# Moving the overflow branch, the router's order and three smaller edits in a two-layer attention and expert kernel

## The chip, the cores and the metric

The kernel runs on one core of a Trainium2 chip. The metric is the device time of one execution in microseconds. A core has five engines that run their own instruction streams and wait for each other through semaphores: TensorE (PE in the rows; PEld are its weight loads, which overlap the products), VectorE (DVE), ScalarE (ACT), GpSimd (POOL) and SyncE (SP), which here only issues DMA transfers. A `q` behind an engine's name (SPq, PEldq) marks an instruction of that engine's sequencer: a DMA issue, a register load, a branch, a semaphore.

## The reference, cut to what matters

512 tokens of 1024 numbers go through two layers. Each layer is a mixer (two kinds of attention and an output projection) and a mixture of 16 experts, each followed by a layer norm:

```python
for l in range(DEPTH):                        # 2
    mix = hybrid_mixer(x, w_in[l], ...)
    x = layer_norm(ALPHA * x + mix, ln1_g[l], ln1_b[l])
    ffn = grouped_moe(x, router_w, router_bias, w_gate[l], w_up[l], w_down[l])
    x = layer_norm(ALPHA * x + ffn, ln2_g[l], ln2_b[l])
# grouped_moe
aff = sigmoid(xt @ router_w)                  # 512 x 16
biased = aff + router_bias
group_score = sum of the two largest of biased in each of 4 groups of 4 experts
g_sel = argmax(group_score); e_idx = the two largest of biased inside group g_sel
gates = aff at e_idx, divided by their sum
out = sum over experts of gates * (silu(xt @ w_gate) * (xt @ w_up)) @ w_down
```

## The kernel before, in words

Most of the kernel is written for a planner that orders each engine's instructions by the order in which they are traced, takes a later one where an engine would otherwise be free, and draws the semaphores. Two places are ordered by hand with `tc.manual_schedule`: the end of the mixer and router (lines 764 to 817, for VectorE, ScalarE and TensorE) and the end of a layer.

**Router.** The tokens are four tiles of 128. For tile t, `residual` adds the mixer's output, `turn` transposes the sum through TensorE, and `logits` (line 652) multiplies it with the router's weights in eight steps of 128 rows, two half tiles of four steps; each float32 step shows as two records. `wgb` holds the router's weights, 16 columns of a step beside 16 columns of another product. `scores` finishes the logits with mean and deviation (L695, L696). `route` (line 860) chooses on VectorE, for two tiles at once, the group and the two experts (L885 to L914, many small operations that depend on each other), and counts the tokens ahead of each with small TensorE products (L921); `R["pos"]` (L924) is each token's place in its expert's list. `centre` and `scaled` (L689, L701) write the normed rows x1, which are stored to DRAM (`xdr`). `places` makes, from the positions, a matrix that picks expert 0's tokens, and `gather(t, i)` (L722) collects, transposed, half i of the columns of expert 0's rows out of tile t by TensorE. All four tiles of a half must be in before the half is complete. Twelve small products (`warm`, L200) have no use but to keep TensorE at work.

**Overflow.** An expert's list holds 128 tokens. `route_count` takes the largest position, over partitions by a TensorE transposition, into an integer `cmi`. `overflow` (line 1170) loads it into a register of every engine (L1172) and branches (L1175) over a loop that would compute the surplus tokens; with these inputs the loop is skipped. On the skipping path each engine increments its own semaphores by what the skipped code would have done, and SyncE does so for the semaphores of eight DMA lanes.

**Experts.** For each of 16 experts `gate_up` multiplies 128 gathered rows with the gate and up weights in eight pieces. The weights come by SyncE in loads of 1 MB (`load_gu` four, `load_wd` two per expert) into 12 `big` buffers. ScalarE copies each piece to a rounded part (L163) and VectorE subtracts to get the rest (L164, for expert 0 also L731 and L736 in `first_hi` and `first_lo`), into four `hl` buffers; each piece then takes three pairs of products (L1061, L1062). `down` (L1083) does the same with the down weights. `between` holds what is traced ahead of a piece. Rows of experts from 1 on are gathered by GpSimd (`fetch`, an indirect DMA, L1025) into `xg`, from lists made by `listed` and `index`, and are transposed and split by `rows_T`. Results of experts 0 to 12 are scattered to DRAM (`ydr`). Those of experts 13 to 15 (`LATE` = 13) stay on the chip; `late_rows` prepares their way back and multiplies out the gates of the expert's tokens (L1119), read by L1122. `parts` (L1092, L1093) takes a late expert's result out of its banks. The eight PSUM banks have three names: four `mm`, two `tr`, two `pv`. The down-projection uses two `pv`, one for each half of the columns.

What stands between the router and the experts before:

```python
fetch(1)
with tc.issue_after(r["counted"]):      # the cast of the count
    pre["lo"](2); pre["lo"](3)
with tc.manual_schedule(engines={SP}):
    overflow(l, r)
    pre["gu", 2] = load_gu(l, 2)
```

Of the kernel before, what the change touches and what calls it, by code (L numbers as in the profile page):

```python
# [8 lines left out]
F32 = mybir.dt.float32  # L9
# [5 lines left out]
OP = mybir.AluOpType  # L15
# [80 lines left out]
def block_kernel(ctx, tc, xT0, x0, win, wqk, wuv, wo, gvec, lnp, rw, rb, wgu, wdn, consts, angles, stripd, rowsd, out):  # L96
# [36 lines left out]
    def u4(name, dt=F32):  # L133
        return sl.tile([128, 1024], dt, name=name, tag="u4", bufs=NU4)
# [18 lines left out]
    def ps(tag):  # L153
        return psp.tile([128, 512], F32, name=tag, bufs={"mm": 4, "tr": 2, "pv": 2}[tag])
# [3 lines left out]

    nlo = [0]

    def split(hi, lo, src, eng=None):

        i = nc.scalar.copy(hi, src).ins  # L163
        (eng or nc.vector).tensor_sub(lo, src, hi.bitcast(F32))  # L164
        return i
# [65 lines left out]
    def attention(l, xh, xl, wraw, first, rest, x_dram):  # L231
# [373 lines left out]

        wgb = u4("wgb")[:, :256].rearrange("p (a b c) -> p a b c", a=8, b=2)
        for j in range(2):
# [44 lines left out]
        def logits(t, i):  # L652

            if i == 0:
                pls[t] = ps("pv")
            for k in range(4 * i, 4 * i + 4):
                R["pe"] = nc.tensor.matmul(pls[t][:, :NE], xts[t][i][:, (k % 4) * 128:(k % 4 + 1) * 128],
                                           wgb[:, k, 0, :], start=(k == 0), stop=(k == 7)).ins

# [38 lines left out]
        def scaled(t, a, b_):  # L698
            c = slice(a * 512, b_ * 512)
            x1 = pre["x1"][t]  # L700
            nc.vector.scalar_tensor_tensor(x1[:, c], x1[:, c], rss[t], b[:, c], op0=OP.mult, op1=OP.add)  # L701
            if b_ == 2:
                (nc.sync if t == NT - 1 else nc.scalar).dma_start(xdr[l][t * 128:(t + 1) * 128, :], x1)

        def norm(t):
# [58 lines left out]
        with tc.manual_schedule(engines={E.DVE, E.Activation, E.PE}):  # L764
# [18 lines left out]
            turn(3, 0)  # L783
            R["warm"] = ps("tr")
            turn(3, 1)
            logits(3, 0)
            gather(0, 0)
            logits(3, 1)
            scores(2)
            centre(3, 0, 1)  # L790
            scores(3)
            first_hi(2)
            centre(3, 1, 2)
            gather(0, 1)
            gather(1, 0)
            gather(1, 1)
            warm(6, R["warm"], R["pe"])

# [8 lines left out]
            places(3)  # L807
            cm = route_count(R)
            scaled(2, 1, 2)
            scaled(3, 0, 1)  # L810
            scaled(3, 1, 2)
            gather(2, 0)
            gather(2, 1)
            cm()
            gather(3, 0)
            gather(3, 1)
# [9 lines left out]
    def load_gu(l, e, part=None, after=None):  # L826
        ws = []
        for k in range(4) if part is None else (part,):
            w = bigt()
            i = nc.sync.dma_start(w, wgu[l, e, :, 2048 * k:2048 * (k + 1)]).ins  # L830
            if after is not None:
                tc.add_manual_dep(i, after.name, mybir.DependencyInfo(mybir.DependencyClass.Sync,
                                                                      mybir.DependencyReason.DATA),
                                  reason="small transfers first")
            ws.append(w)
        return ws if part is None else ws[0]
# [23 lines left out]
    def route(R, lg, ta, tb, while_placing=lambda: None):  # L860
# [16 lines left out]
        def v16(t):  # L877
# [14 lines left out]
        gs = st(G)  # L892
        nc.vector.reduce_max(gs, pr, axis=AX.X)
        gs4 = gs.rearrange("p (t g) -> p t g", t=n)
        mx = st(n)
        nc.vector.reduce_max(mx, gs4, axis=AX.X)
        ge = st(G)
        ge4 = ge.rearrange("p (t g) -> p t g", t=n)
        nc.vector.tensor_tensor(ge4, gs4, mx[:, :, None].to_broadcast([128, n, 4]), op=OP.is_equal)
        nc.vector.tensor_mul(ge, ge, C("gw", 0, G))  # L900
        nc.vector.reduce_max(mx, ge4, axis=AX.X)
        nc.vector.tensor_tensor(ge4, ge4, mx[:, :, None].to_broadcast([128, n, 4]), op=OP.is_equal)

# [3 lines left out]
        bi = b4[:, :, None, :].to_broadcast([128, G, 4, 4])  # L907
        nc.vector.tensor_tensor(v4(t1), bi, bj, op=OP.is_ge)
        nc.vector.tensor_tensor(v4(t2), bi, bj, op=OP.is_gt)
        nc.vector.tensor_mul(v16(t1), v16(t1), lt)  # L910
        nc.vector.tensor_max(t1, t1, t2)
        rk = st()
        nc.vector.reduce_sum(rk, t1.rearrange("p (a b) -> p a b", b=4), axis=AX.X)
        nc.vector.scalar_tensor_tensor(sel.rearrange("p (g j) -> p g j", j=4), rk.rearrange("p (g j) -> p g j", j=4),  # L914
                                       1.5, ge[:, :, None].to_broadcast([128, G, 4]), op0=OP.is_lt, op1=OP.mult)
# [11 lines left out]
    def route_count(R):  # L927

        cm = sm.tile([128, 2], F32, name="cs")
        nc.vector.reduce_max(cm[:, 0:1], R["pos"], axis=AX.X)  # L930

        def over_tokens():
            pm = ps("tr")
            nc.tensor.transpose(pm[0:1, 0:128], cm[:, 0:1], ident)
            nc.vector.reduce_max(cm[0:1, 1:2], pm[0:1, 0:128], axis=AX.X)
            R["counted"] = nc.vector.tensor_copy(R["cmi"][0:1], cm[0:1, 1:2]).ins

        return over_tokens

# [40 lines left out]
    def ffn_plain(l, e, xg):  # L980


        def piece(w, k):
            t = u4("wp")
            nc.sync.dma_start(t, w[l, bass.ds(e, 1), :, k * 1024:(k + 1) * 1024].rearrange("o p m -> p (o m)"))
            return t
# [22 lines left out]
    def experts(l, r, pre):  # L1009
# [100 lines left out]
        def late_rows(e):  # L1110
# [5 lines left out]
            nc.scalar.copy(ohT, transpose4(of, 0))  # L1116
            p = ps("pv")
            for t in range(NT):
# [5 lines left out]

        fetch(1)
        with tc.issue_after(r["counted"]):
            pre["lo"](2)
            pre["lo"](3)
        with tc.manual_schedule(engines={mybir.EngineType.SP}):
            overflow(l, r)  # L1130
            pre["gu", 2] = load_gu(l, 2)
        st[0] = {}
        rows_T(0, 0)
        rows_T(0, 1)
        for e in range(NE):
# [12 lines left out]
            if e == 1:  # L1148
                between[4] = lambda: fetch(3)
            if e and e + 3 < NE:  # L1150
# [19 lines left out]
    def overflow(l, r):  # L1170
# [4 lines left out]
        with tc.If(cnt > CAP):  # L1175
# [15 lines left out]
            with tc.For_i(0, NE, 1) as e:  # L1191
                oe = sm.tile([128, 1], F32, name="o_oe", bufs=1)
                with tc.For_i(0, NT, 1) as t:
                    nc.sync.dma_start(oe, od[bass.ds(e, 1), :, bass.ds(t, 1)].rearrange("o p m -> p (o m)"))
                    oi = sm.tile([128, 1], I32, name="o_oi", bufs=1)
                    nc.vector.tensor_copy(oi, oe)
                    xr = u4("xr")
                    nc.sync.dma_start(xr, xdr[l].rearrange("(t p) d -> t p d", p=128)[bass.ds(t, 1)].rearrange(
# [294 lines left out]
```

## Time and profile before

| what | value |
|---|---|
| three timed runs | median 1224.01 us (1220.31 to 1225.26) |
| profiled execution | 1224.46 us, span 1222.7 us |
| TensorE busy | 1160.0 us, 95% |
| VectorE, ScalarE, GpSimd busy | 84%, 66%, 24% |
| mean granted clock of TensorE | 0.974 |
| HBM | 267.96 MB read, 31.98 MB written |

All times in rows are microseconds from the start of the span unless marked ns. In a timeline row stand the start, the duration, the engine, the line, the operation, the tiles written and read (out<-in) and their shapes; neighbours of one kind are merged and counted (x8). In brackets is the idle time of the engine before, and what ended it. A granted clock of 1.00 is the level of 2.4 GHz, 0.50 that of 1.2 GHz. The ends of matmuls are modelled.

### The profile page before, as it was taken

Reading aid. Unit: us, or ns where it says so; the run is one execution under the profiler, and the core shown is the slowest. Engines: PE = TensorE matmul, PEld = TensorE weight load, DVE = VectorE, ACT = ScalarE, POOL = GpSimd, SP = SyncE. Lnnn points to the kernel's source line nnn. Section 1 sums busy time; section 2 is a strip of 40 time slices with the busy share of each in tenths; the row PEclk is TensorE's granted clock in tenths of the full one; section 3 lists DMA queues with packets and bytes.
Section 4 is the critical chain, followed back from the end, with each engine's and each line's share of the span. In section 5 each row is a group of like instructions: output and inputs, shape, how many; then the busy total and the mean of one; then the engine's idle time right before and its main releaser. Section 6 shows DMA issues by size and latency. Waiting matters only on the chain. (4 is left out here: it accounts for less than half of the span.)

```text
span 1222.7 us, 16875 instructions
## 1 busy us (share of the span) xinstructions
PE 1160.0 (95%) x5753; PEld 910.2 (74%) x5753; DVE 1027.7 (84%) x1859; ACT 802.6 (66%) x1264; POOL 298.5 (24%) x237
## 2 busy tenths in 40 slices
PE   8998899999999999999898998999989999999995
PEld 6686556787788888887686765568878888888873
DVE  4599967488999999988957998665789999999887
ACT  4533668344888888887545346773448888888873
POOL 2336332210111111200543443322102111112004
PEclk8999999998999999999999999999889999999998
DMA  7626004465999999987236160145479999999741
GB/s 253 199 71 231 29 18 147 162 226 231 377 380 389 390 376 381 373 325 282 87 130 175 50 237 1 70 138 184 161 291 378 391 380 393 382 372 365 293 172 69
DMA packets 56972, 292.21 MB, mean 239 GB/s; under 512 B 10063, under 2 KB 13903, under 8 KB 28464
## 3 DMA queue, kind: packets, MB, share of 16 engines
q1 hardware_dynamic: 47376, 270.48, 60.0%
q0 software_dynamic: 8064, 15.36, 3.5%
q10 hardware_dynamic: 1440, 5.24, 1.1%
q8 instruction: 47, 0.77, 0.3%
q14 instruction: 45, 0.37, 0.1%
HBM read 267.96 MB, written 31.98 MB: 245 GB/s over the span
## 5 line engine op out<-in xcount | busy, mean ns | idle before, releaser
L163 ACT CAST hl<-big 128x1024 fp32r<-128x1024 f32 x438 | 457.6, 1054 | 126.8 <-PE mm L1062 62.3
L164 DVE TENSOR_TENSOR hl<-big,hl 128x1024 fp32r<-128x1024 f32 x403 | 484.6, 1226 | 58.2 <-ACT hl L163 51.0
L1061 PE MATMUL mm<-hl,xh 128*128 128x512 f32 x504 | 207.4, 412 | 0.0
L1062 PE MATMUL mm<-hl,xh 128*128 128x512 f32 x504 | 197.4, 392 | 0.0
L1083 PE MATMUL pv<-hl,hT 128*128 128x512 f32 x720 | 172.6, 395 | 4.1 <-DVE big L1093 4.1
L1083 PEld LDWEIGHTS pv<-hl,hT 128*128 128x128 f32 x720 | 136.7, 190 | 33.7 <-DVE big L1093 4.8
L271 PE MATMUL mm<-big,hl 128*128 128x512 f32 (+1 forms) x624 | 142.7, 387 | 2.3 <-ACT hl L163 1.2
L271 PEld LDWEIGHTS mm<-big,hl 128*128 128x128 f32 x624 | 114.4, 195 | 28.0 <-ACT hl L163 2.9
L1025 POOL DMA_INDIRECT xg<-xdr,ii x30 | 52.4, 1746 | 288.2 <-DVE ii L1039 254.0
L164 POOL TENSOR_TENSOR hl<-big,hl 128x1024 fp32r<-128x1024 f32 x35 | 84.7, 2424 | 134.4 <-ACT hl L163 120.1
L1062 PEld LDWEIGHTS mm<-hl,xh 128*128 128x128 f32 x504 | 95.4, 189 | 16.0
L1061 PEld LDWEIGHTS mm<-hl,xh 128*128 128x128 f32 x504 | 95.2, 189 | 15.7
L1062 PE MATMUL mm<-hl,xl 128*128 128x512 f32 x252 | 98.8, 392 | 0.0
L1061 PE MATMUL mm<-hl,xl 128*128 128x512 f32 x252 | 98.7, 392 | 0.0
L633 PE MATMUL mm<-hl,big 128*128 128x512 f32 x384 | 94.6, 397 | 0.0
L492 ACT ACTIVATE P<-P,mn 128x128 f32<-128x128 f32 (+3 forms) x128 | 71.9, 568 | 18.6 <-DVE mn L490 16.5
L633 PEld LDWEIGHTS mm<-hl,big 128*128 128x128 f32 x384 | 70.3, 188 | 13.3
L504 ACT COPY big<-tr 128x512 f32<-128x512 f32 (+3 forms) x128 | 49.7, 431 | 36.5 <-PE tr L502 35.5
L502 PE MATMUL tr<-cn,P 128*128 128x128 f32 x320 | 61.8, 293 | 9.8 <-DVE P L498 9.3
L502 PEld LDWEIGHTS tr<-cn,P 128*128 128x128 f32 x320 | 36.0, 141 | 42.8 <-ACT big L504 17.1
L1103 POOL DMA_INDIRECT ydr<-y,ii x26 | 26.5, 1018 | 146.8 <-ACT y L1099 123.2
L572 POOL TENSOR_TENSOR mh<-dd,cn 128x256 f32<-128x256 f32 (+2 forms) x64 | 44.5, 717 | 66.1 <-DVE mn L490 39.8
(277 smaller groups left out, 1881.7 us busy)
## 6 DMA issues: line engine op xcount, KB each, us to landing
big<-wgu SPq DMA_DIRECT2D x128, 1024.0 KB, 7.6
big<-wdn SPq DMA_DIRECT2D x64, 1024.0 KB, 7.1
big<-win SPq DMA_DIRECT2D x10, 1024.0 KB, 5.6
ydr<-zz SPq DMA_DIRECT2D x2, 4096.0 KB
big<-wo SPq DMA_DIRECT2D x8, 1024.0 KB, 9.8
big<-ydr SPq DMA_DIRECT2D x8, 1024.0 KB, 4.9
big<-wqk SPq DMA_DIRECT2D x4, 1024.0 KB, 6.1
big<-dq SPq DMA_DIRECT2D x32, 128.0 KB, 2.3
```

Source lines behind the costliest of these rows:

```text
L163: i = nc.scalar.copy(hi, src).ins
L164: (eng or nc.vector).tensor_sub(lo, src, hi.bitcast(F32))
L271: nc.tensor.matmul(p[:, ts], w[j == 1][:, k * 128:(k + 1) * 128], x, start=(j + k == 0), stop=(j == end and k == 7))
L492: nc.scalar.activation(e, e, AF.Exp, bias=mn[:, i:i + 1], scale=-1.0, accum_out=su[:, i:i + 1])
L502: nc.tensor.transpose(p[:, (i - kb) * 128:(i - kb + 1) * 128], P[:, PO[i] + kb * 128:PO[i] + (kb + 1) * 128], ident)
L504: copies.append(nc.scalar.copy(pt[kb], p[:, :512 - 128 * kb]).ins)
L572: last_mask[0] = nc.gpsimd.tensor_tensor(m[:, c:c + w], dd, C("slope", h, h + 1).to_broadcast([128, w]), op=OP.mult)
L633: R["pe"] = nc.tensor.matmul(pp[t][i], x, w[:, i * 512:(i + 1) * 512], start=first, stop=last).ins
L1025: return nc.gpsimd.indirect_dma_start(out=st[e]["xg"], out_offset=None, in_=xdr[l], in_offset=bass.IndirectOffsetOnAxis(ap=st[e]["ii"][:, ...
L1061: nc.tensor.matmul(pg, x, w[:, :512], start=(k == 0 and x is a and w is wh), stop=last)
L1062: nc.tensor.matmul(pu, x, w[:, 512:], start=(k == 0 and x is a and w is wh), stop=last)
L1083: nc.tensor.matmul(py[i], x, w[:, i * 512:(i + 1) * 512], start=(k == 0 and x is a and w is wh), stop=last)
```

## The change

- Overflow: the branch moves from between router and experts into expert 14 (`LATE + 1`), ahead of piece 3 of its gate and up products. The count is taken ahead of piece 3 of expert 0.
- Router's products: `logits` multiplies with 128 columns instead of 16. The columns beyond the 16 wanted are those of neighbouring steps and zeros, and nobody reads their results; the zeros are set by GpSimd.
- Order of the router's end: the gather of tile 0's first half goes behind all logits, tile 1's second half behind the routing; `centre(3)` is one operation; the warm-up products go; the last gathers finish the first half of columns before the second.
- `route`: the same operations, with those that choose the group and those that rank the experts alternating.
- Second expert's gather: three of the four loads of the third expert's gate and up weights wait until GpSimd has issued the gather of expert 1 (`issued`, a small memset behind it). `first_lo` of pieces 2 and 3 goes behind the split of expert 0's rows.
- Rows of expert 1 are transposed ahead of piece 7 of expert 0 and piece 1 of expert 1 (before: 6 and 7).
- Gates' product in `late_rows`: bank `mm` instead of `pv`.
- Inside the branch: one weight buffer, and the scratch tile for the rows.

```diff
     def split(hi, lo, src, eng=None):
         i = nc.scalar.copy(hi, src).ins
-        (eng or nc.vector).tensor_sub(lo, src, hi.bitcast(F32))
+        last_lo[0] = (eng or nc.vector).tensor_sub(lo, src, hi.bitcast(F32)).ins
...
-        wgb = u4("wgb")[:, :256].rearrange("p (a b c) -> p a b c", a=8, b=2)
+        wgt = u4("wgb")
+        wgb = wgt[:, :256].rearrange("p (a b c) -> p a b c", a=8, b=2)
+        nc.gpsimd.memset(wgt[:, 256:384], 0.0)
...
-                R["pe"] = nc.tensor.matmul(pls[t][:, :NE], xts[t][i][:, (k % 4) * 128:(k % 4 + 1) * 128],
-                                           wgb[:, k, 0, :], start=(k == 0), stop=(k == 7)).ins
+                R["pe"] = nc.tensor.matmul(pls[t][:, :128], xts[t][i][:, (k % 4) * 128:(k % 4 + 1) * 128],
+                                           wgt[:, 32 * k:32 * k + 128], start=(k == 0), stop=(k == 7)).ins
...
             turn(3, 0)
-            R["warm"] = ps("tr")
             turn(3, 1)
             logits(3, 0)
-            gather(0, 0)
             logits(3, 1)
             scores(2)
-            centre(3, 0, 1)
+            centre(3)
             scores(3)
             first_hi(2)
-            centre(3, 1, 2)
+            gather(0, 0)
             gather(0, 1)
             gather(1, 0)
-            gather(1, 1)
-            warm(6, R["warm"], R["pe"])
...
             places(2)
             places(3)
-            cm = route_count(R)
+            scaled(3, 0, 1)
             scaled(2, 1, 2)
-            scaled(3, 0, 1)
+            gather(1, 1)
             scaled(3, 1, 2)
             gather(2, 0)
+            gather(3, 0)
             gather(2, 1)
-            cm()
-            gather(3, 0)
             gather(3, 1)
...
-        nc.vector.reduce_max(gs, pr, axis=AX.X)
...
         nc.vector.tensor_tensor(v4(t1), bi, bj, op=OP.is_ge)
+        nc.vector.reduce_max(gs, pr, axis=AX.X)
         nc.vector.tensor_tensor(v4(t2), bi, bj, op=OP.is_gt)
+        nc.vector.reduce_max(mx, gs4, axis=AX.X)
         nc.vector.tensor_mul(v16(t1), v16(t1), lt)
+        nc.vector.tensor_tensor(ge4, gs4, mxb, op=OP.is_equal)
         nc.vector.tensor_max(t1, t1, t2)
+        nc.vector.tensor_mul(ge, ge, C("gw", 0, G))
...
-            p = ps("pv")
+            p = ps("mm")
             for t in range(NT):
                 nc.tensor.matmul(p[:, 0:1], of[:, t * 128:(t + 1) * 128], r["gm"][:, t * NE + e:t * NE + e + 1],
...
-        fetch(1)
-        with tc.issue_after(r["counted"]):
-            pre["lo"](2)
-            pre["lo"](3)
-        with tc.manual_schedule(engines={mybir.EngineType.SP}):
-            overflow(l, r)
-            pre["gu", 2] = load_gu(l, 2)
+        fetched = fetch(1)
+        with tc.issue_after(fetched):
+
+            issued = nc.gpsimd.memset(sm.tile([128, 1], F32, name="gs"), 0.0)
         st[0] = {}
         rows_T(0, 0)
         rows_T(0, 1)
+        with tc.issue_after(last_lo[0]):
+            pre["lo"](2)
+            pre["lo"](3)
+        pre["gu", 2] = [load_gu(l, 2, k, issued if k else None) for k in range(4)]
...
-                between[5 if e else 6] = lambda: rows_T(e + 1, 0)
-                between[6 if e else 7] = lambda: rows_T(e + 1, 1)
+                between[5 if e else 7] = lambda: rows_T(e + 1, 0)
+                if e:
+                    between[6] = lambda: rows_T(e + 1, 1)
             if LATE - 1 <= e < NE - 1:
                 between[3] = lambda: late_rows(e + 1)
+            if e == LATE + 1:
+                between[3] = both(lambda: overflow(l, r), between[3])
             if e == 0:
+                between[3] = lambda: route_count(r)
                 between[4] = lambda: (route_rest(r), index(1, 1, 2))
-                between[6] = both(lambda: (listed(0), index(0, 1, 2)), between[6])
-                between[7] = both(lambda: fetch(2), between[7])
+                between[6] = lambda: (listed(0), index(0, 1, 2))
+                between[7] = both(between[7], lambda: fetch(2))
             if e == 1:
+                between[1] = lambda: rows_T(1, 1)
                 between[4] = lambda: fetch(3)
```

## Rows read from the trace of the kernel before

**Rows 1.** The page: busy us by engine; a costly group (busy, mean ns | idle before).

```profile
PE 1160.0 (95%) x5753; PEld 910.2 (74%) x5753; DVE 1027.7 (84%) x1859; ACT 802.6 (66%) x1264; POOL 298.5 (24%) x237
...
L164 DVE TENSOR_TENSOR hl<-big,hl 128x1024 fp32r<-128x1024 f32 x403 | 484.6, 1226 | 58.2 <-ACT hl L163 51.0
```

**Rows 2.** Waits of TensorE: us in total, times, longest.

```profile
PE mm L1061 <- ACT xh L163: 5.9, 2, 4.0
```

**Rows 3.** Timeline of layer 0, from tile 3's logits to expert 0.

```profile
273.08 1.06 PE L657 MATMUL pv<-wgb,xt 128*128 128x16 f32 x8 [0.24 <-ACT xt L650]
...
274.00 1.76 PE L722 MATMUL mm<-oh,x 128*128 128x128 f32 x8
...
277.32 0.23 DVE L695 SCALAR_TENSOR_TENSOR lg<-c,lnm,pv 128x16 f32<-128x16 f32 x1 [3.40 <-PE pv L657]
...
278.69 0.18 DVE L889 TENSOR_TENSOR route<-route 128x24 f32<-128x24 f32 x1
...
281.56 0.19 DVE L914 SCALAR_TENSOR_TENSOR r_sel<-route 128x32 bf16<-128x32 f32 x1
...
281.80 1.47 PE L200 MATMUL tr<-strip 128*128 128x256 bf16 x12
...
283.52 0.19 DVE L924 TENSOR_TENSOR r_pos<-pv,r_sel 128x32 f32<-128x32 f32 x1 [1.11 <-PE pv L921]
...
284.09 2.14 PE L722 MATMUL mm<-oh,x 128*128 128x128 f32 x16 [0.61 <-DVE oh L716]
...
289.42 1.07 ACT L163 CAST xh<-mm 128x512 fp32r<-128x512 f32 x2 [8.82 <-SPq L1175]
...
290.06 0.50 PE L1061 MATMUL mm<-big,xh 128*128 128x512 f32 x1 [1.90 <-ACT xh L163]
```

**Rows 4.** Timeline of layer 1, tile 3's logits and expert 0's first product.

```profile
877.60 1.10 PE L657 MATMUL pv<-wgb,xt 128*128 128x16 f32 x8 [0.24 <-ACT xt L650]
...
896.63 0.80 PE L1061 MATMUL mm<-big,xh 128*128 128x512 f32 x1 [3.96 <-ACT xh L163]
```

**Rows 5.** Stretches: length, busy us (instructions) by engine, granted clock, DMA share, GB/s.

```profile
270.90:274.30 3.40, 3.16 (x28) 2.92 (x28) 2.81 (x8) 1.85 (x3) 0.92 (x1) 1.00 0.95 304
274.30:281.20 6.90, 6.90 (x35) 6.90 (x34) 3.54 (x18) 2.81 (x5) 0.00 (x0) 0.51 0.02 5
284.60:288.00 3.40, 3.40 (x33) 3.35 (x32) 3.37 (x8) 0.00 (x0) 0.00 (x0) 1.00 0.62 248
291.30:294.80 3.50, 3.50 (x10) 2.67 (x10) 3.50 (x11) 1.08 (x2) 0.00 (x0) 0.51 0.95 371
...
895.50:902.40 6.90, 5.77 (x14) 4.47 (x15) 5.63 (x15) 2.96 (x4) 0.73 (x1) 0.51 0.79 297
```

**Rows 6.** Timeline of VectorE, routing of the first two tiles of layer 0.

```profile
257.61 0.17 DVE L889 TENSOR_TENSOR route<-route 128x24 f32<-128x24 f32 x1
...
259.30 0.15 DVE L901 TENSOR_REDUCE route<-route 128x2 f32<-128x8 f32 x1
```

**Rows 7.** Timeline of the stages of experts 14 and 15, layers 0 and 1.

```profile
560.85 4.61 PE L1083 MATMUL pv<-hl,hT 128*128 128x512 f32 x12 [2.06 <-DVE big L1093]
...
568.82 0.15 DVE L1122 COPY gs<-pv 128x1 f32<-128x1 f32 x1
...
576.18 2.89 PE L1083 MATMUL pv<-hl,hT 128*128 128x512 f32 x12
...
1167.10 4.23 PE L1083 MATMUL pv<-hl,hT 128*128 128x512 f32 x12 [2.06 <-DVE big L1093]
```

**Rows 8.** Branch lines: duration ns min/median/max, first and last start us.

```profile
L1172 PEldq TENSOR_LOAD <-r_cmi x2: 926/1006/1087, 287.1 to 891.9; - x2
...
L1175 PEldq COMPARE_BRANCH  x2: 328/340/352, 288.3 to 892.9; - x2
```

**Rows 9.** DMA issues of the page: KB each, median us to landing.

```profile
big<-wdn SPq DMA_DIRECT2D x64, 1024.0 KB, 7.1
```

**Rows 10.** Waits of SyncE's queue: us in total, times, longest.

```profile
SPq L830 <- DVE hl L164: 251.4, 88, 17.8
```

More of the change, by code (lines that the diff above doesn't have):

```diff
@@ L157, in bigt @@
         return big.tile([128, 2048], dt, name="big")
-    nlo = [0]
+    nlo, last_lo = [0], [None]
     def split(hi, lo, src, eng=None):
         i = nc.scalar.copy(hi, src).ins
-        (eng or nc.vector).tensor_sub(lo, src, hi.bitcast(F32))
+        last_lo[0] = (eng or nc.vector).tensor_sub(lo, src, hi.bitcast(F32)).ins
         return i
@@ L700, in scaled @@
             x1 = pre["x1"][t]
-            nc.vector.scalar_tensor_tensor(x1[:, c], x1[:, c], rss[t], b[:, c], op0=OP.mult, op1=OP.add)
+            i = nc.vector.scalar_tensor_tensor(x1[:, c], x1[:, c], rss[t], b[:, c], op0=OP.mult, op1=OP.add).ins
             if b_ == 2:
                 (nc.sync if t == NT - 1 else nc.scalar).dma_start(xdr[l][t * 128:(t + 1) * 128, :], x1)
+            return i
         def norm(t):
@@ L831, in load_gu @@
             if after is not None:
-                tc.add_manual_dep(i, after.name, mybir.DependencyInfo(mybir.DependencyClass.Sync,
+                tc.add_manual_dep(i, after.ins.name, mybir.DependencyInfo(mybir.DependencyClass.Sync,
                                                                       mybir.DependencyReason.DATA),
-                                  reason="small transfers first")
+                                  reason="rows first")
             ws.append(w)
@@ L892, in route @@
         gs = st(G)
-        nc.vector.reduce_max(gs, pr, axis=AX.X)
         gs4 = gs.rearrange("p (t g) -> p t g", t=n)
-        mx = st(n)
-        nc.vector.reduce_max(mx, gs4, axis=AX.X)
-        ge = st(G)
+        mx, ge = st(n), st(G)
         ge4 = ge.rearrange("p (t g) -> p t g", t=n)
[L899 to L902, printed above, removed]
+        mxb = mx[:, :, None].to_broadcast([128, n, 4])
         t1, t2 = st(4 * W), st(4 * W)
@@ L908, in route @@
         nc.vector.tensor_tensor(v4(t1), bi, bj, op=OP.is_ge)
+        nc.vector.reduce_max(gs, pr, axis=AX.X)
         nc.vector.tensor_tensor(v4(t2), bi, bj, op=OP.is_gt)
+        nc.vector.reduce_max(mx, gs4, axis=AX.X)
         nc.vector.tensor_mul(v16(t1), v16(t1), lt)
+        nc.vector.tensor_tensor(ge4, gs4, mxb, op=OP.is_equal)
         nc.vector.tensor_max(t1, t1, t2)
+        nc.vector.tensor_mul(ge, ge, C("gw", 0, G))
         rk = st()
         nc.vector.reduce_sum(rk, t1.rearrange("p (a b) -> p a b", b=4), axis=AX.X)
+        nc.vector.reduce_max(mx, ge4, axis=AX.X)
+        nc.vector.tensor_tensor(ge4, ge4, mxb, op=OP.is_equal)
         nc.vector.scalar_tensor_tensor(sel.rearrange("p (g j) -> p g j", j=4), rk.rearrange("p (g j) -> p g j", j=4),
@@ L930, in route_count @@
         nc.vector.reduce_max(cm[:, 0:1], R["pos"], axis=AX.X)
[L932 to L938, printed above, removed]
+        pm = ps("tr")
+        nc.tensor.transpose(pm[0:1, 0:128], cm[:, 0:1], ident)
+        nc.vector.reduce_max(cm[0:1, 1:2], pm[0:1, 0:128], axis=AX.X)
+        nc.vector.tensor_copy(R["cmi"][0:1], cm[0:1, 1:2])
     def second(a2, t1, sel):
@@ L980, in ffn_plain @@
     def ffn_plain(l, e, xg):
+        t = u4("wp")
         def piece(w, k):
-            t = u4("wp")
             nc.sync.dma_start(t, w[l, bass.ds(e, 1), :, k * 1024:(k + 1) * 1024].rearrange("o p m -> p (o m)"))
@@ L1196, in overflow @@
                     nc.vector.tensor_copy(oi, oe)
-                    xr = u4("xr")
+                    xr = scr
                     nc.sync.dma_start(xr, xdr[l].rearrange("(t p) d -> t p d", p=128)[bass.ds(t, 1)].rearrange(
```

## The prediction

> **What bounds the kernel now.** I read the busy times first, then TensorE's waits, then the timeline and the granted clock of the two places that the change touches, in both layers. TensorE is busy 1160.0 of 1222.7 us [rows 1]; all its gaps together are some 63 us, so a gain must come from a named gap or from a stretch at the low clock. In the waits the reader is to see that its longest single wait is 4.0 us, for ScalarE's copy of the first expert's rows; it comes once per layer [rows 2]. The timeline of layer 0 shows its cause: the gathers run from 284.09, then the count is taken, every engine goes through the overflow branch, and ScalarE's copy is released by SyncE's semaphores of that branch (L1175) at 289.42; expert 0's products start at 290.06 after 1.90 us of nothing [rows 3]. In layer 1 the same gap is 3.96 us, up to 896.63 [rows 4]. The granted clock is 0.51 (the 1.2 GHz level for nearly all of it) from 274.3 to 281.2 and again after each gap, from 291.3 and from 895.5; in between, over the gathers from 284.6, it is 1.00 [rows 5].
>
> **The change, part by part.** The sum is made against the profiled execution's own 1224.46 us (span 1222.7), which is 0.45 above the median shown.
>
> Router, both layers. Now: eight records of tile 3's first logits from 273.08, a gather of eight records at 0.22 us each (low clock), the other logits, so that VectorE's L695 starts at 277.32 [rows 3]. The gather goes behind the logits, so these start at 274.0. What 128 columns cost: eight 16-wide records take 1.06 us, sixteen 128-wide gather records 2.14 [rows 3], 0.133 against 0.134 each; the weight loads set the pace in both. Below, the difference could be zero, above, 0.01 us for each of the 64 records of a layer; I take 0.3 us a layer, 0.6 in all. The clock I take as full here, because the 128-wide gathers of 284.6 to 288.0 kept it full while the stretch before the fall, 3.16 of 3.40 us busy but largely 16-wide, did not [rows 5]. Then the logits end at 274.0 + 8 x 0.13 = 275.1.
>
> The Trainium skill, "TensorE: Matmul & The Clock Gate", section "What's actually happening", lets the clock follow how busy the engine has been. Read as busy time, that speaks against the widening: the engine was busy before the fall as well. By it the low clock stays at the router, and that is the first rival, priced below from rows.
>
> L695 to L889 is 1.37 us today [rows 3] and stays so. L889 to the end of L914 is 3.06 [rows 3], with each dependent step waiting for the last. The new order alternates two chains; the scheduler already did so in the first half's routing, where L889 to L901 took 1.69 us [rows 6]. With two more steps of 0.2 and the last one's 0.19, 2.28. So the selection is ready at 275.1 + 0.05 + 1.37 + 2.28 = 278.8 instead of 281.75. TensorE has meanwhile done 24 gather records (3.1 us, to 278.2) and waits some 0.6. Today the counting products come behind the warm-up products, which end at 283.27, and the positions (L924) at 283.52 [rows 3]; then they come 0.6 after the selection, at 279.4. The gather moved behind the routing fills the 0.57 that today lies between L924 and the first gather [rows 3], and takes 1.05 in all, to 280.5; four more gathers of eight records take 4.2, to 284.7. Both gathers of the first half of columns come first, so ScalarE's copy and VectorE's subtraction of that half run beside the other two. Nothing waits for the branch, so expert 0 starts at 284.7 instead of 290.06: 5.4 us. Layer 1 repeats the rows 604.5 us later (877.60 against 273.08), so 889.2 instead of 896.63: 7.4 us [rows 3, 4]. Together 12.8.
>
> Clock behind it. With no gap of 1.9 or 3.96 us the clock has no reason in these rows to fall. The stretch from 291.3 (3.50 us busy at half speed) gives back 1.7, that from 895.5 (5.77 busy) 2.9: 4.6 [rows 5].
>
> Gates' product in another bank. In expert 14 twelve products of the down-projection wait 2.06 us for VectorE's L1093 and then take 4.61; the same twelve an expert later take 2.89 [rows 7]. They wait because the gates' product of expert 15 holds one of the two "pv" banks until L1122 reads it at 568.82 [rows 7]; the down-projection had one bank for both halves. Among four "mm" banks, of which the gate and up products hold two, nothing has to wait for it. Gain 2.06 + 1.72 in layer 0 and 2.06 + 1.34 in layer 1: 7.2 us.
>
> Branch in expert 14. It now stands in TensorE's full stream. TensorE's register load takes 1.01 us and its compare and branch 0.34 [rows 8], after which it waits for its own queue to run empty. At best the queue covers this (0), without cover it is 1.35 and a restart: I take 1.5 a layer, 3.0 in all, since the load begins at 287.1, while the second sixteen of the gather records from 284.09 still run [rows 3, 8], but the queue's depth is not shown. SyncE also waits there for the loads in flight; behind it stand expert 15's down weights and the loads of the other experts' results, none needed before expert 14's down-projection, which starts at 576.18 [rows 7], some 30 us on; ScalarE and VectorE wait for SyncE only where they reuse a buffer that the branch writes. The upper end is the second rival. The count's four small operations go beside expert 0's products.
>
> Start of the experts. Two subtractions of weights (1.23 us each) [rows 1] leave the dead time and go behind the rows' own, on a VectorE that is full in these stretches (3.37 of 3.40, 3.50 of 3.50) [rows 5]; the next expert's rows are turned one and two weight pieces later than now. What is late next is split weights or rows. The trace has no such wait at a start without the gap; below, it could be nothing, above, the 2.46 of both subtractions. I take 1.5 a layer, nearer to the upper end because VectorE is full, 3.0 in all. The second gather and VectorE's lists for it move up with the router. Three of the third expert's four loads wait for GpSimd to have issued that gather; behind them in SyncE's queue stand the down weights of expert 1 and the loads of expert 3, all of use an expert or more later, so I cost the order at nothing; without that cover it is one load, 7.1 us to land [rows 9]. The memsets fall on GpSimd, 24% busy [rows 1]. The single buffer inside the branch runs only if the branch is taken.
>
> Sum: 12.8 + 4.6 + 7.2 = 24.6 gained, 0.6 + 3.0 + 3.0 = 6.6 given back, net 18.0: 1224.46 - 18.0 = 1206.5, forecast 1206.
>
> **Rivals.**
> 1. The clock stays low at the router. For: it fell with TensorE nearly fully busy [rows 5]. Against: the gathers kept it up. Eight logit records and 24 gather records then take 0.22 each, to 281.1; positions at 281.7, five gathers, start at 286.9 instead of 284.7: 2.2 a layer, 1211.
> 2. The branch is dear. SyncE can leave it only when its loads have landed, 7.1 us for one of 1 MB [rows 9]; ScalarE's copy of the next rows waits for it, as it does today [rows 3], and the weights' copies queue behind. With two pieces of split weights in hand (12 products, 2.7 us) TensorE stands 4.4 and loses 1.7 to the clock: 6.1 a layer instead of 1.5, 9.2 more, 1216. Against: SyncE may come to the branch long before TensorE.
> 3. VectorE becomes the bound in the first experts. The dead time gave it the 2.4 of the two subtractions, the low clock behind it about 2.3 us a layer (half of 4.6); if it needs them all, 4.7 instead of 1.5 a layer, 6.4 more: 1213. For: rows 5. Against: splits stood ahead of their use.
> 4. Slower than before: SyncE reaches the branch behind a load that waits for a buffer. The longest such wait is 17.8 us [rows 10]; ScalarE waits for SyncE, less 2.7 in hand, plus 1.7 of clock: 16.8 a layer instead of 1.5, 30.6 more: 1237. It decides from 10.5 us a layer ((18.0 + 3.0) / 2). Against: what stands ahead of the branch by program order is loads of earlier need.
>
> **Chances.** Forecast 0.48, rival 1 0.17, rival 2 0.13, rival 3 0.17, rival 4 0.05. The range takes in 1, 2 and 3 at their prices; below, the unknown costs at zero (6.6 less, to 1200) and two more for stretches of low clock that fall elsewhere: 1198 to 1216. A measurement of this kernel tells 0.5% (6.1 us) from no change, so faster means under 1217.9: the first four cases but for 0.07 of them that overrun their prices, 0.88; same 0.07; slower 0.05.
>
> **What would show it.** Right: no TensorE gap over 0.7 us between the last gather and expert 0; clock 1.00 over logits and gathers of tile 3, and over expert 0's first products; start of expert 0 about 11.6 us after tile 3's first logits (17.0 and 19.0 now); no wait of L1083 for L1093; the branch's rows in expert 14 with a TensorE gap of 1 to 2 us. Wrong: PEclk still 0.5 at the router (rival 1); ScalarE waiting for SyncE's branch line in expert 14 (2, 4); waits of L1061 for L164 in experts 0 and 1 (3).

## The result, and the profile after

| | median us (lowest to highest) | profiled execution, span |
|---|---|---|
| before, four runs | 1224.4 (1220.31 to 1225.26) | 1224.46, 1222.7 |
| after, four runs | 1211.28 (1207.42 to 1213.77) | 1213.77, 1212.0 |

The ratio of after to before is 0.9897 (95% interval 0.9862 to 0.9931): 13 us faster, inside the range of 1198 to 1216, where 18 were forecast. The profiled execution of after is the slowest of its four and 10.7 us under the profiled one of before; the accounts below are of these two.

The page's busy times, to set beside [rows 1]:

```profile
PE 1150.3 (95%) x5729; PEld 901.6 (74%) x5729; DVE 1026.7 (85%) x1857; ACT 802.6 (66%) x1264; POOL 303.4 (25%) x241
```

TensorE's waits. The wait of [rows 2] is gone; in its place stand a wait of the counting products (L919) for the choice of experts, one of expert 1's and expert 2's transpositions for gathered rows, and one of expert 0's down products (L1078) for split weights:

```profile
PE pv L919 <- DVE r_sel L912: 6.2, 4, 2.3
...
PE tr L190 <- DMA xg<-xdr,ii: 2.2, 3, 1.1
...
PE pv L1078 <- DVE hl L164: 0.8, 2, 0.4
```

The timeline of layer 0 from tile 3's logits to expert 0, against [rows 3]:

```profile
275.59 2.05 PE L659 MATMUL pv<-wgb,xt 128*128 128x128 f32 x16 [0.24 <-ACT xt L652]
...
277.48 2.84 PE L725 MATMUL mm<-oh,x 128*128 128x128 f32 x24
...
280.91 0.19 DVE L912 SCALAR_TENSOR_TENSOR r_sel<-route 128x32 bf16<-128x32 f32 x1
...
281.16 0.27 PE L919 MATMUL pv<-r_sel,strip 128*128 128x16 bf16 x5 [0.76 <-DVE r_sel L912]
...
281.28 4.81 PE L725 MATMUL mm<-oh,x 128*128 128x128 f32 x40
...
286.00 0.48 PE L1056 MATMUL mm<-big,xh 128*128 128x512 f32 x1
```

No gap stands between the last gather and expert 0, and behind the logits one of 0.76 us is left. From the first of these logits to expert 0 it is 10.41 us (before 16.98). The windows, with the columns of [rows 5], show the clock in the mix, over the router, and in the late experts of both layers:

```profile
255.50:261.60 6.10, 4.93 (x17) 3.94 (x18) 5.59 (x17) 1.99 (x2) 0.00 (x0) 0.72 0.31 126
274.30:281.20 6.90, 5.90 (x56) 5.58 (x55) 5.49 (x26) 4.67 (x7) 0.92 (x1) 1.00 0.69 286
...
281.20:286.00 4.80, 4.80 (x48) 4.77 (x48) 4.56 (x14) 0.58 (x1) 0.00 (x0) 1.00 0.29 117
...
551.80:555.20 3.40, 3.40 (x13) 2.83 (x11) 1.38 (x2) 1.18 (x2) 0.00 (x0) 0.50 0.96 354
1152.50:1155.90 3.40, 3.40 (x14) 3.01 (x14) 1.51 (x3) 1.30 (x3) 0.00 (x0) 0.50 0.97 357
```

The clock is full over the router, where it was 0.51 [rows 5]; it falls at 258 in the mix, where it had not, and behind the branch in expert 14.

A stretch that the forecast did not look at lost time: the first half's routing inside the mix. Its timeline (layer 0):

```profile
249.33 5.02 PE L635 MATMUL mm<-hl,big 128*128 128x512 f32 x21
...
251.27 2.98 POOL L164 TENSOR_TENSOR hl<-big,hl 128x1024 fp32r<-128x1024 f32 x1 [0.74 <-ACT hl L163]
...
251.91 2.38 DVE L883 SCALAR_TENSOR_TENSOR route<-r_gm,rbt 128x32 f32<-128x32 f32 x1
...
256.42 0.19 DVE L912 SCALAR_TENSOR_TENSOR r_sel<-route 128x32 bf16<-128x32 f32 x1
...
256.67 0.23 PE L919 MATMUL pv<-r_sel,strip 128*128 128x16 bf16 x3 [2.32 <-DVE r_sel L912]
```

TensorE reaches the counting products 21 mix products behind tile 1's logits and waits 2.32 us. In the trace of before 39 products stood between, and the wait was 0.35:

```profile
252.49 9.11 PE L633 MATMUL mm<-hl,big 128*128 128x512 f32 x39
252.81 2.41 POOL L164 TENSOR_TENSOR hl<-big,hl 128x1024 fp32r<-128x1024 f32 x1 [0.59 <-ACT hl L163]
253.02 2.24 DVE L696 SCALAR_TENSOR_TENSOR lg<-lg,lny,c 128x16 f32<-128x16 f32 x1
...
261.95 0.22 PE L921 MATMUL pv<-r_sel,strip 128*128 128x16 bf16 x3 [0.35 <-DVE r_sel L914]
```

The branch in expert 14:

```profile
548.38 0.39 PE L1057 MATMUL mm<-hl,xh 128*128 128x512 f32 x1
...
549.32 0.35 PE L1114 MATMUL mm<-r_gm,of 128*128 128x1 f32 x2 [0.55 <-ACT h L971]
...
550.21 0.66 PE L190 MATMUL tr<-cn,of 128*128 128x128 f32 x4 [0.53 <-ACTq L1176]
...
551.29 1.52 PE L190 MATMUL tr<-cn,xg 128*128 128x128 f32 x8
...
552.47 2.06 PE L1078 MATMUL pv<-hl,hT 128*128 128x512 f32 x4
```

All gate and up products of expert 14 lie ahead of the branch, and everything narrow of expert 15 (gates' product, transposed lists and rows) behind it, in one piece of 4 us with two gaps, before the down products at 552.47. The low clock follows at 551.8. TensorE waited for ScalarE at both gaps, not for SyncE: SyncE's own branch (L1176) ran at 535.7, TensorE's at 546.3.

Between starts of products on TensorE, in us, layer 0 / layer 1 (M: first product of the mix to expert 0's first; X: from there to expert 1's first down product; E: expert 12's first down product to expert 14's):

| kernel | ratio to before (95%) | M | X | E |
|---|---|---|---|---|
| before | 1 | 78.28 / 80.31 | 46.43 / 45.90 | 39.99 / 40.09 |
| after | 0.9897 | 75.30 / 73.66 | 46.12 / 46.08 | 38.81 / 38.82 |
| e1 bank only | 0.9940 (0.9918 to 0.9962) | 78.25 / 77.27 | 46.42 / 45.36 | 35.84 / 35.91 |
| e2 branch only | 0.9971 (0.9951 to 0.9992) | 76.20 / 76.22 | 46.71 / 45.97 | 38.99 / 39.14 |
| e3 width only | 1.0017 (0.9998 to 1.0037) | 78.04 / 79.54 | 46.42 / 45.59 | 39.86 / 39.86 |
| e4 wide late | 0.9860 (0.9832 to 0.9887) | 71.74 / 71.80 | 45.98 / 45.71 | 37.24 / 37.24 |
| e5 no branch | 0.9814 (0.9791 to 0.9836) | 71.75 / 71.75 | 46.21 / 45.79 | 35.84 / 35.84 |
| e6 branch behind rows | 0.9848 (0.9830 to 0.9866) | 71.72 / 71.73 | 46.16 / 45.61 | 37.57 / 37.57 |
| e7 branch in 15 | 0.9806 (0.9785 to 0.9827) | 71.73 / 71.73 | 45.53 / 45.88 | 36.24 / 36.24 |
| e8 all narrow | 0.9853 (0.9834 to 0.9871) | 73.99 / 73.88 | 45.99 / 45.68 | 37.24 / 37.24 |
| e9 old route | 0.9850 (0.9824 to 0.9876) | 72.48 / 72.50 | 46.10 / 45.67 | 36.24 / 36.31 |
| e10 loads free | 0.9883 (0.9857 to 0.9908) | 71.74 / 71.74 | 50.39 / 48.99 | 36.24 / 36.24 |
| e11 rows early | 0.9887 (0.9863 to 0.9912) | 71.75 / 71.74 | 48.54 / 50.68 | 36.31 / 36.24 |
| e12 counts held | 0.9808 (0.9795 to 0.9822) | 71.23 / 71.21 | 45.75 / 45.96 | 36.31 / 36.24 |

The stages are read from one execution each; the ratios are over several. What no edit touches differs too: the start to the first mix product took 209.4 to 213.0 us, and from layer 0's join of the late experts to layer 1's mix 228.8 to 231.6, with stretches of low clock in other places. A total is therefore good for some 4 us in a single execution. The stages repeat better where their edits are the same (M is 71.7 to 71.8 in both layers of e4, e5, e6, e7, e10 and e11), and they tell the edits apart. One stage does not: M of layer 1 is 80.31 in before and 77.27 in e1, which edits nothing there; the clock over the router, low in before, was full in e1 (below).

### The profile page after: what moved, and what is told of

Read it like the earlier page. It is cut to its first block, busy times and chain, and to the rows that moved or that the text cites. A ratio compares the mean times of both kernels' runs of the same rounds, so it can differ in the third digit from the quotient of the medians.

```text
span 1212.0 us, 16822 instructions
## 1 busy us (share of the span) xinstructions
PE 1150.3 (95%) x5729; PEld 901.6 (74%) x5729; DVE 1026.7 (85%) x1857; ACT 802.6 (66%) x1264; POOL 303.4 (25%) x241
## 5 line engine op out<-in xcount | busy, mean ns | idle before, releaser
L164 DVE TENSOR_TENSOR hl<-big,hl 128x1024 fp32r<-128x1024 f32 x403 | 483.5, 1226 | 49.7 <-ACT hl L163 42.9
L1056 PE MATMUL mm<-hl,xh 128*128 128x512 f32 x504 | 206.7, 410 | 0.0
L1078 PE MATMUL pv<-hl,hT 128*128 128x512 f32 x720 | 172.0, 394 | 0.8 <-DVE hl L164 0.8
L1078 PEld LDWEIGHTS pv<-hl,hT 128*128 128x128 f32 x720 | 136.4, 190 | 30.0 <-DVE hl L164 1.7
L164 POOL TENSOR_TENSOR hl<-big,hl 128x1024 fp32r<-128x1024 f32 x35 | 85.9, 2458 | 134.1 <-ACT hl L163 118.8
L1056 PEld LDWEIGHTS mm<-hl,xh 128*128 128x128 f32 x504 | 94.8, 188 | 16.2 <-ACT hl L163 0.3
L1056 PE MATMUL mm<-hl,xl 128*128 128x512 f32 x252 | 98.8, 392 | 0.0
```

Of the source, the lines that this page charges most:

```text
L164: last_lo[0] = (eng or nc.vector).tensor_sub(lo, src, hi.bitcast(F32)).ins
L1056: nc.tensor.matmul(pg, x, w[:, :512], start=(k == 0 and x is a and w is wh), stop=last)
L1078: nc.tensor.matmul(py[i], x, w[:, i * 512:(i + 1) * 512], start=(k == 0 and x is a and w is wh), stop=last)
```

## The experiments

The theory after this reading: the router, the clock there and the bank gained what was forecast or more; the loss in the mix comes from the new width moving the counting products forward, and the branch costs by what it pushes behind itself. The rival for the mix: VectorE's slow operation beside GpSimd makes the wait, wherever the products stand.

**e1, the bank alone** (kernel before)

```diff
-            p = ps("pv")
+            p = ps("mm")
```

> Kernel before with one edit: the gates' product of the late experts takes a bank of the four-bank pool instead of the two-bank pool. My theory (the forecast's own term): the two waits of TensorE in the late experts (3.8 and 3.4 us after the scaling of expert 12's and 13's output) go and nothing comes in their place while the branch is not there: 1224 - 7.2 = 1217 (1215 to 1219). Rival: in the changed kernel the late experts gained only 1.2 us a layer because the next wait is right behind the one removed, whatever the branch does: 1221 to 1223, with new gaps of TensorE before expert 13's and 14's down products.

1214.72 us against 1222.84. Down products of experts 13 and 14 in layer 0:

```profile
555.85 5.60 PE L1083 MATMUL pv<-hl,hT 128*128 128x512 f32 x24
...
572.64 2.89 PE L1083 MATMUL pv<-hl,hT 128*128 128x512 f32 x12
```

The wait for L1093 is gone without a successor, 4.15 and 4.18 us in E: the theory's term, 8.3 us instead of 7.2. In layer 1 of this execution the narrow router ran at the full clock:

```profile
876.00:883.00 7.00, 6.84 (x64) 6.63 (x65) 4.52 (x21) 3.85 (x6) 0.00 (x0) 1.00 0.13 55
```

So the clock does not fall at the narrow products every time, and 3.0 us of this run's M in layer 1 are not the bank's.

**e2, the branch alone** (kernel before, branch in expert 14 with its one weight buffer and scratch tile; the count stays at the router)

```diff
-            overflow(l, r)
             pre["gu", 2] = load_gu(l, 2)
...
+            if e == LATE + 1:
+                between[3] = both(lambda: overflow(l, r), between[3])
```

> Kernel before with the overflow branch alone moved into expert 14 (as the changed kernel has it), all else as before, the products of the router 16 columns wide and the gates' product in the old bank. Theory: the branch by itself held expert 0 back, so the start of expert 0 comes earlier by some 5 us a layer, and the branch costs 1 to 1.5 us a layer in expert 14: 1224 - 10 + 3 = 1217 (1214 to 1219). Rival: the clock's fall in the router belongs to the narrow products and stays, and with the route's old order VectorE ends late: 1220 to 1223.

1219.40 us, between the two. M gains 2.1 and 4.1 only. The clock over the router (layer 0):

```profile
272.20:279.00 6.80, 6.80 (x35) 6.80 (x33) 3.44 (x18) 2.80 (x5) 0.00 (x0) 0.50 0.37 153
```

So the branch alone does not free the router: the clock falls there without the branch's gap too.

**e3, the width alone** (kernel before, `wgt` as in the change)

```diff
-                R["pe"] = nc.tensor.matmul(pls[t][:, :NE], xts[t][i][:, (k % 4) * 128:(k % 4 + 1) * 128],
-                                           wgb[:, k, 0, :], start=(k == 0), stop=(k == 7)).ins
+                R["pe"] = nc.tensor.matmul(pls[t][:, :128], xts[t][i][:, (k % 4) * 128:(k % 4 + 1) * 128],
+                                           wgt[:, 32 * k:32 * k + 128], start=(k == 0), stop=(k == 7)).ins
```

> Kernel before with the router's products 128 columns wide in all four tiles and nothing else. Theory: the width alone moves the first half's counting products from behind 39 to behind 21 products of the mix in TensorE's order, where they wait 2.3 us for the choice of experts in each layer; the clock at the router of tiles 2 and 3 stays high, which gives back up to 1.7 us a layer: 1222 to 1229, with a wait of 2.3 us ahead of the counting products in both layers. Rival: the wait in the changed kernel comes from VectorE (an operation of 2.4 us beside GpSimd) and not from the order: then no new wait shows, and the time is 1220 to 1223.

1223.42 us against 1222.84: no change. Both parts of the theory show, the wait of the counting products (here L923) and the full clock over the router (layer 0):

```profile
PE pv L923 <- DVE r_sel L916: 5.6, 4, 2.3
```

```profile
271.50:286.90 15.40, 13.88 (x126) 13.24 (x125) 12.42 (x43) 4.84 (x8) 1.42 (x2) 1.00 0.33 119
```

**e4, wide in tiles 2 and 3 only** (kernel after)

```diff
-                R["pe"] = nc.tensor.matmul(pls[t][:, :128], xts[t][i][:, (k % 4) * 128:(k % 4 + 1) * 128],
-                                           wgt[:, 32 * k:32 * k + 128], start=(k == 0), stop=(k == 7)).ins
+                n = 128 if t > 1 else NE
+                R["pe"] = nc.tensor.matmul(pls[t][:, :n], xts[t][i][:, (k % 4) * 128:(k % 4 + 1) * 128],
+                                           wgt[:, 32 * k:32 * k + n], start=(k == 0), stop=(k == 7)).ins
```

> Changed kernel, but the router's products are 128 columns wide only in tiles 2 and 3 and 16 wide in tiles 0 and 1. Theory: the order of the first half is that of before (counting products behind 39 products of the mix), the waits of 2.3 us in each layer go, and with the one in layer 0 the fall of the clock behind it (1.7 us): 1211.3 - 4.6 - 1.7 = 1205 (1203 to 1208). Rival: the waits stay, since VectorE's slow operation sets them, or go to the next place: 1210 to 1213.

1204.41 us. The first half's counting products stand behind 39 mix products again, and the four waits of the counting products, two in each layer, are

```profile
PE pv L920 <- DVE r_sel L913: 2.2, 4, 0.8
```

M is 3.6 and 1.9 shorter than after. Expert 14 is unedited, yet E is 1.57 shorter: here the clock did not fall behind the branch, so that part of E in after does not follow from the order of the instructions.

**e5, no branch** (e4 with the call of `overflow` left out, and with it the surplus tokens, which these inputs do not have)

> The kernel of e4 (wide products in tiles 2 and 3 only) without the overflow branch in either layer: the part left out is the handling of experts with more than 128 tokens, which these inputs never enter. Theory: what the branch still costs is the difference of experts 13 and 14 between e4 and e1, 37.24 against 35.84 us a layer: 1204.4 - 2.8 = 1201.6 (1200 to 1203). Rival: the branch also holds SyncE's loads behind it, so that late loads return more than that: below 1199. Second rival: TensorE's gaps at the branch are only moved to the next wait: 1203.5 to 1205.

1200.76 us. E is 1.40 a layer shorter than in e4: 2.8 us for the branch, against the forecast's 3.0.

**e6, the branch behind expert 15's rows** (e4)

```diff
-            if e == LATE + 1:
-                between[3] = both(lambda: overflow(l, r), between[3])
+            if e == LATE + 1:
+                between[7] = lambda: overflow(l, r)
```

> The kernel of e4 with the branch behind the turning of expert 15's rows and its gates' product (ahead of expert 14's last granule instead of its fourth). Theory: the branch's two banks and its place in the order pushed that narrow work behind all of expert 14's products; with the branch behind it the work lies between the products again, and only TensorE's own stop at the branch (some 0.5 us a layer) is left: 1204.4 - 1.8 = 1202.6 (1201 to 1204). Rival: the stop is the price, wherever the branch stands: 1204 to 1206.

1206.52 us: the expectation failed. The narrow work does lie between the products again, but E is 0.33 longer than in e4. The last gate and up product and the first down product:

```profile
548.44 0.39 PE L1058 MATMUL mm<-hl,xh 128*128 128x512 f32 x1
550.27 0.96 PE L1079 MATMUL pv<-hl,hT 128*128 128x512 f32 x3 [1.44 <-ACTq L1177]
```

TensorE stops for ScalarE's passage through the branch, 1.44 us, where e4 had two gaps of 0.6 and 0.5 us. The rival, that the stop is the price wherever the branch stands, is near this run and falls with the next.

**e7, the branch in expert 15** (e4)

```diff
-            if e == LATE + 1:
-                between[3] = both(lambda: overflow(l, r), between[3])
+            if e == NE - 1:
+                between[3] = lambda: overflow(l, r)
```

> The kernel of e4 with the branch in expert 15 instead of expert 14, where no rows of a later expert are left to turn. Theory: nothing can bunch behind the branch, its stop on TensorE lies between wide products: 1204.4 - 1.8 = 1202.6 (1201 to 1204). Rival: so late, its stop delays the loads of the combine that SyncE issues behind it, or ScalarE and VectorE at the last expert's end: 1205 to 1209.

1200.78 us, as without a branch. Around it on TensorE:

```profile
561.27 0.39 PE L1057 MATMUL mm<-hl,xl 128*128 128x512 f32 x1
...
561.81 0.47 PE L1058 MATMUL mm<-hl,xl 128*128 128x512 f32 x1
```

The starts are 0.54 us apart instead of 0.23: 0.3 us is the stop, and E is 0.40 longer than in e5. That the products behind it find split weights ready, while in e6 they need ScalarE, is read from the two orders, not tried apart.

**e8, all products narrow** (kernel after)

```diff
-                R["pe"] = nc.tensor.matmul(pls[t][:, :128], xts[t][i][:, (k % 4) * 128:(k % 4 + 1) * 128],
-                                           wgt[:, 32 * k:32 * k + 128], start=(k == 0), stop=(k == 7)).ins
+                R["pe"] = nc.tensor.matmul(pls[t][:, :NE], xts[t][i][:, (k % 4) * 128:(k % 4 + 1) * 128],
+                                           wgb[:, k, 0, :], start=(k == 0), stop=(k == 7)).ins
```

> The changed kernel with the router's products 16 columns wide in all four tiles, as before. Theory: the width of tiles 2 and 3 keeps TensorE's clock at 2.4 GHz through the router; without it the clock falls there in both layers as in the branch-only run (6.8 us at half clock at 272 and 876), and expert 0 starts some 2 us later in each layer than in e4: 1204.4 + 4 = 1208.5 (1206 to 1211). Rival: with the branch gone and the route's order changed the gap is short enough that the clock stays up, and the narrow products are shorter by 0.3 us a tile: 1203 to 1204.5.

1207.38 us; M is 2.2 and 2.1 longer than in e4, with

```profile
274.40:281.20 6.80, 6.80 (x34) 6.80 (x34) 4.02 (x21) 3.10 (x5) 0.00 (x0) 0.50 0.40 164
```

over the router, and 0.50 in layer 1 as well. By stages the width of tiles 2 and 3 is worth 4.3 us; the ratios of e4 and e8 overlap and do not show it. Over all runs the clock was 1.00 over each of the twenty routers with wide products in tile 3, and low over seven of the eight with narrow ones; the eighth is e1's layer 1.

**e9, the old order of `route`** (e7, the two chains one behind the other)

> The kernel of e7 (wide products in tiles 2 and 3 only, branch in expert 15) with the router's small operations on VectorE in the order of before, each behind the one whose result it needs. Theory: the alternation shortens the chain from the first of them to the choice of experts from 3.28 us (branch-only run) to 2.56 us (e7), and the second half's counting products wait for it: TensorE's wait there grows from 0.76 to about 1.5 us in each layer, 1.4 us slower than e7's ratio of 0.9806, that is 0.9818. Rival: the first half's choice gets late too and TensorE's clock falls in the longer wait: 0.984 or more. Second rival: nothing waits for it: the same as e7.

1206.25 us. The wait is 0.75 longer in the second half of each layer,

```profile
PE pv L920 <- DVE r_sel L913: 3.7, 4, 1.5
```

and M 0.76 longer: 1.5 us, as the theory has it. The profiled executions differ by 6.2 us (1206.25 against 1200.02); of the other 4.7 the two untouched stages named above hold 4.1 (444.0 against 439.9 us together), so the ratio overstates this edit.

**e10, the third expert's loads free of the gather** (e7)

```diff
-        pre["gu", 2] = [load_gu(l, 2, k, issued if k else None) for k in range(4)]
+        pre["gu", 2] = load_gu(l, 2)
```

> The kernel of e7 with the third expert's gate and up loads issued without waiting for the second expert's gather. Theory: the four loads of 1 MB are then in the queues ahead of the gather's rows, the rows of expert 1 land later than 7.8 to 9.5 us after their issue, and TensorE waits for them in expert 0 more than e7's 0.6 to 0.9 us, by 2 us or more in a layer: 1204 at e7's 1200.8. Rival: the loads wait for free buffers anyway, and the order on the queues is unchanged: the same as e7 within 1 us.

1209.35 us. X is 4.9 and 3.1 longer; expert 1's gather lands 11.5 us (layer 0) and 10.3 us (layer 1) after its issue, against 5.4 and 5.5 in e7, and TensorE waits for its rows (e7: 1.5 us in two waits):

```profile
PE tr L190 <- DMA xg<-xdr,ii: 6.5, 2, 4.0
```

**e11, expert 1's rows turned early** (e7, ahead of pieces 6 and 7 of expert 0, with the list and the gather of expert 2 back in their old order)

> The kernel of e7 with the turning of expert 1's rows back ahead of expert 0's seventh and eighth granule, instead of ahead of the eighth and of expert 1's second. Theory: with the second expert's gather ahead of the loads the rows land at 20 us after the start of expert 0 at the latest, so the turning waits for them in front of expert 0's last products: 1 to 2 us a layer slower than e7 (1202 to 1205). Rival: the later turning only put the narrow work into expert 1, whose output is late by the same 1.4 us (18 to 19.4 us from its down products to the next): the same as e7 or 1 to 3 us faster.

1210.21 us, more than expected: X is 3.0 and 4.8 longer, with waits and a stretch at half clock behind them in each layer (0.52 from 295.8 to 299.2, 0.50 from 905.0 to 908.5).

```profile
PE tr L190 <- DMA xg<-xdr,ii: 5.1, 3, 2.9
```

**e12, all products wide, counting products held back** (kernel after, branch as in e7)

```diff
-                    route(R, lg, 0, 2)
-                    places(0)
-                    places(1)
+                    counts = route(R, lg, 0, 2), s   # counting part returned
...
+            if counts and s == counts[1] + 4:
+                with tc.issue_after(R["pe"]):
+                    counts[0]()
+                places(0)
+                places(1)
```

> The changed kernel with its wide products in all four tiles, the branch in expert 15 as in e7, and the first half's counting products held back until 43 products of the mix are issued behind tile 1's products (instead of 21). Theory: the loss in the mix is the place of the counting products alone; with them held back their wait (2.3 us in each layer) goes though the products stay wide, the way from the mix's start to expert 0's start is 71.6 to 72.2 us as in e7 (71.7) instead of 73.7 (layer 1 of the changed kernel), and the time is that of e7, a ratio of 0.979 to 0.983. Rival: the wide products of tiles 0 and 1 cost the time themselves, or the choice of experts reaches its users late: 73 us or more from the mix to expert 0, a ratio of 0.984 or more.

1200.37 us. The wait in the mix is gone though every product is wide, and though VectorE's operation there still takes 2.40 us; the two waits left are those of the second half:

```profile
249.22 10.02 PE L635 MATMUL mm<-hl,big 128*128 128x512 f32 x43
...
251.80 2.40 DVE L887 SCALAR_TENSOR_TENSOR route<-r_gm,rbt 128x32 f32<-128x32 f32 x1
...
259.08 0.23 PE L924 MATMUL pv<-r_sel,strip 128*128 128x16 bf16 x3
```

```profile
PE pv L924 <- DVE r_sel L916: 1.5, 2, 0.8
```

M is 71.2, the shortest of all. This settles the mix: whether TensorE waits is decided by the place of the counting products, at any width and with VectorE's slow operation still there. How long it waits in the early place is that operation's doing: 2.19 of its 2.38 us are more than it takes elsewhere, and the wait in after is 2.32 (an account from rows, not tried apart). e7 and e12 are 23 to 24 us faster than before and some 11 faster than the change.

## Why the prediction was near, and where it missed

Profiled pair, span: 10.7 us gained where 18.0 were forecast.

- **Router.** Forecast 12.8 less 0.6 for the width; measured 16.98 to 10.41 and 19.03 to 10.41, together 15.2. The mechanism came, and the times in it were priced too long. The forecast spanned 11.6 us from the logits, with the choice of experts ready at 5.7, 0.6 from there to the gathers and 5.25 for forty records; in after these are 5.51, 0.18 and 4.72. TensorE's wait for the choice was priced at 0.6 and is 0.76. Rival 1 did not come: with 128 columns the clock is 1.00 (0.51 in [rows 5]). What the Trainium skill, "TensorE: Matmul & The Clock Gate", section "What's actually happening", says, that the clock follows how busy the engine has been, does not agree with these runs when it is read as busy time: the narrow router of e8 is busy 6.80 of 6.80 us at 0.50. Part of the 15.2 is luck: 3.0 us of before's 19.03 in layer 1 are the low clock over the narrow router, which e1 did not have (16.01 there). No part gives the gain alone: the branch alone (e2) and the width alone (e3) left M at 76 and 78 us or more, both with the new order reach 71.7 (e4); the new order alone was not taken back.
- **Step missed: the mix.** "128 columns" was priced at 0.01 us a record, and the first half's logits only by that. The width changed what the planner put where, and that cost 3.6 us in layer 0, with low clock behind the wait, and 2.0 in layer 1: 5.6, the largest part of the shortfall. e3, e4 and e12 show it.
- **Bank.** Forecast 7.2, by e1 8.3. The mechanism came; where the other 1.1 lies was not tried.
- **Branch.** Forecast 1.5 a layer; e4 against e5 gives 1.40. The size was right by luck, for the mechanism named (TensorE's register load and restart) was not it: e7 does all of that for 0.40. In expert 14 narrow work collects behind the branch and waits for ScalarE: the two gaps of 0.55 and 0.53 us are 1.1 of the 1.40. In the profiled run of after 1.57 a layer of low clock came on top, 3.1 in all, for which the sum had no term. Rivals 2 and 4 did not come: SyncE passed the branch ahead of TensorE, and no wait of TensorE was for SyncE.
- **Start of the experts.** Forecast 4.6 regained from the clock less 3.0; the low stretches at 291.3 and 895.5 are gone, but X changed by -0.31 and +0.18, so about 1.4 and 3.1 were given back. Part of it is in waits for the two things that the forecast named, gathered rows (2.2 us in three waits, before 1.1 in one) and split weights (0.8 in two); the rest was not tried. Rival 3 did not come: TensorE's waits have none of the gate and up products (L1056) for L164. The wait of the third expert's loads was costed at nothing, and no run speaks against that; what it protects had no term in the sum: without it X is 8.0 us longer (e10).
- **Not from the change:** 2.7 us more in layer 1's attention, 1.1 less ahead of the mix. The median, 13.1 under before, lies between the account and the forecast.

## What to carry to other kernels

Where a planner orders the instructions, a change of one operation's size moves its neighbours: read the new order of every engine in that stretch, not only the edited products. A branch that every engine passes was cheap here where wide work with ready operands stood on both sides of it (0.40 us a layer), and dear where the work behind it needed an engine that passed later (1.40 in e4, 1.73 in e6). When a gain is some 10 us in 1200, compare stages between fixed instructions; stretches of low clock elsewhere move the total by several, and they can fall into the stage itself: look at its granted clock in both kernels.

## What the hardware showed

- One small VectorE operation, 0.19 us elsewhere, took 2.38 us in the mix (L883, timeline above). It ended at 254.29, GpSimd's subtraction L164 at 254.25; before, L696 did the same beside the same kind of subtraction (253.02 to 255.26, GpSimd 252.81 to 255.22). The Trainium skill, "SBUF — State Buffer", section "Who interferes with whom", says that a VectorE instruction with two SBUF inputs contends with a GpSimd instruction that reads SBUF and that the later one waits to the end; the two pairs of ends agree.
- Products that keep TensorE busy all the time can run at the low level: 6.80 of 6.80 us busy at 0.50 over the narrow router (e8), 1.00 over the wide one (274 to 286 in after). They need not: the narrow router in layer 1 of e1 ran at 1.00.
